# One attention kernel: mixed pairs written where they are used, and W_out's attention rows loaded and split in smaller steps

## The chip, the core and the metric

The kernel runs on one core of a Trainium2 chip. The core has five engines with an instruction queue each: PE (TensorE, matmuls and transposes), DVE (VectorE), ACT (ScalarE), POOL (GpSimd) and SP (SyncE, which here only issues DMA transfers). Each engine takes its instructions in a fixed order and waits on semaphores for the others. The metric is the time of one execution on the device in microseconds; the median of several runs is given.

## What is computed

One layer of a streaming encoder with 1024 tokens of width 1024, in float32: a feed-forward network (FFN), a token mixer, and a second FFN, each followed by a residual layer norm.

```python
x = layer_norm(ALPHA * x + 0.5 * swiglu(x, ffn1...), ln1_g, ln1_b)
z = x @ w_in                       # q, k, v of 8 heads of 64, the gates, the LRU inputs
fox = forgetting_attention(q, k, v, fg)    # softmax(q.k/8 + cum_t - cum_s) v, causal
lru = gelu(...) * rg_lru(causal_depthwise_conv(...), ...)
mix = concatenate([fox, lru]) @ w_out      # w_out: 1024 x 1024, rows 0..511 belong to fox
x = layer_norm(ALPHA * x + mix, ln2_g, ln2_b)
x = layer_norm(ALPHA * x + 0.5 * swiglu(x, ffn2...), ln3_g, ln3_b)
```

The change touches the attention part: how `fox` is kept until it meets `w_out`, and how the four row blocks of `w_out` that belong to it (128 rows of 1024 each) reach the core.

## The kernel before, in words

**Numbers in two parts.** A float32 operand of a matmul is split in a high part (a cast to the matmul's format, on ACT) and a low part (the difference, on DVE), and each product is three matmuls: high by high, high by low, low by high (`mm3`, lines 166 to 168). So every weight row block costs a cast and a subtraction before PE can use it.

**The attention** (`attention`, from line 1363) runs over 64 units. A unit is one head h and one block i of 128 queries. Heads 0 to 5 run one after the other, i from 7 down to 0; heads 6 and 7 are interleaved at the end. The loop counter n of the program counts units, with a few steps after the last. For each unit, `probs` computes scores on PE (lines 1389, 1390), DVE adds the decay and takes the extremum (1395), ACT the exponential (1396); `to_pT`, three units later (two from unit 32 on), transposes the result on PE (1410) and splits it into `pt` by ACT (1414) and DVE (1415); `values`, for two blocks of queries at a time, multiplies it with v on PE (1431), and ACT and DVE add the two halves into the tile `o` (1434, 1435). From head 5 on (`LAST` = 4), the normalisation is done late: DVE takes the reciprocals (1418), POOL copies them into `gate_raw` (1419), PE transposes them (1440), DVE multiplies (1441). The two heads of a pair together fill 128 rows of `o`, and ACT and DVE (for head 5 POOL) split these into the pair's `mix` tiles, high and low (1443, 1444).

**The other work between the units.** Sixteen fill pieces of 12 matmuls (`piece`) multiply the LRU half of the mix with its rows of W_out; they run at n = 1 to 4 and then three to a head, and the last one at n = 35. At the end come sixteen out tiles (`out_tile`, 12 matmuls each), which multiply the four mixed pairs with the attention rows of W_out, add the residual and normalise; the first comes after the first values of head 7. The stretch from n = 36 to the first out tile has neither.

**W_out's attention rows** are loaded at n = 36 by `out_w` (line 1351): two transfers of 1 MB into the two `raw` buffers, two row blocks each. One whole row block is split at each of n = 39, 41, 43, 45 by `split_ws` (lines 158, 159), 128 x 1024 in one cast and one subtraction.

**The mixed pairs** 0, 1 and 3 are written into two tiles of the pool `mxp`, pair 2 into a tile of the pool `hp`. Pairs 0 and 1 are not left there: when they are complete, POOL stores them to device memory (1447), and at n = 40 and 50 SP loads them into `row` buffers (1532), from which the out tiles read.

**Loads of a head.** At block i = 5 of a head (at (6, 6) for the last) SP asks for the next head's q, k, decay row (1059, 1064) and v (1374). There are two v buffers, so v of head h + 1 takes that of head h - 1, which is still being read by its last values for another unit.

**What sets the order.** A scheduler places the recorded instructions on each engine; `issue_after` makes the issue of a transfer stand behind another one on SP. The pools hand out buffers in turn, and an instruction that writes a buffer waits for the last reader of what was there. The FFN that follows (`ready_pair`) loads weights that were prepared earlier (`pre_d`, line 588): two tiles of operands named t4 and t2 into the two `raw` buffers, and smaller ones into new `ws` buffers that become free when the attention is over.

## Time and profile before

| | |
|---|---|
| median of 3 runs | 2314.07 us (2312.58 to 2314.19) |
| the profiled execution | 2308.6 us, of which the span from first to last instruction 2306.8 us |
| busy: PE, DVE, ACT, POOL | 2278.0, 1701.5, 1063.6, 308.4 us |
| granted PE clock | 0.998 |
| attention, first scores to last out tile | about 1163 to 1379 us of the span |

A row of the timeline has the start in us from the span's begin, the duration, the engine, the line of the kernel, the operation, the tile written and the tiles read, and in brackets the idle time of the engine just before and what ended it. Tile names have no buffer numbers: all `raw` buffers are `raw`. Rows with SPq are transfers issued by SP; a row that covers several instructions (x2) gives the time from the first to the last. PE rows overlap, since matmuls are pipelined: a 128x512 matmul is shown with 0.39 us, and the next starts 0.23 us later.

### The profile page before, as it was taken

To read this page: it belongs to the slowest core of one execution; us is meant where nothing else is said; L and a number is where in the kernel's file an instruction comes from. 1 tells how busy PE (TensorE), PEld (TensorE's weight loads), DVE (VectorE), ACT (ScalarE), POOL (GpSimd) and SP (SyncE) were. 2 spreads that over 40 slices of the span, in tenths; PEclk is the share of its full clock that TensorE was granted. 3 is DMA by queue.
4 is the path that set the end of the run, shared out by engine and by line. 5 is a ranking of instruction groups with operands and counts; after the bars stand their busy time and mean duration, and the time that the engine had idled before them with its cause. 6 is when DMAs were issued, how large, how long until landed. Compare 5 with 4: busy or idle time off the path is not lost.

```text
span 2306.8 us, 29448 instructions
## 1 busy us (share of the span) xinstructions
PE 2278.0 (99%) x10609; PEld 1895.0 (82%) x10609; DVE 1701.5 (74%) x2749; ACT 1063.6 (46%) x1771; POOL 308.4 (13%) x503
## 2 busy tenths in 40 slices
PE   9999999999999999999999999999999999999998
PEld 7878888888888888987788788888888888888887
DVE  8878787878467788877767899665656666577886
ACT  5454545454344335455556755333333343344341
POOL 0242323232000001121133200000000000000000
PEclk9999999999999999999999999999999999999999
DMA  4565656565376444366786734232323232564542
GB/s 155 194 212 210 211 207 216 200 223 188 108 271 221 148 142 149 131 205 203 263 249 165 246 119 151 87 119 87 119 87 119 87 119 87 201 251 159 185 144 73
DMA packets 210321, 387.10 MB, mean 168 GB/s; under 512 B 13616, under 2 KB 112240, under 8 KB 210176
## 3 DMA queue, kind: packets, MB, share of 16 engines
q1 hardware_dynamic: 173760, 262.21, 34.8%
q0 software_dynamic: 36416, 123.02, 13.6%
q8 instruction: 83, 1.36, 0.2%
q14 instruction: 62, 0.51, 0.1%
HBM read 258.27 MB, written 126.91 MB: 167 GB/s over the span
## 4 chain that ended last, share of the span: by engine, by line
PE 87%; DVE 4%; issue 4%; DMA 1%; ACT 1%; POOL 1%; SPq 0%; DVEq 0%; POOLq 0%; ACTq 0%
PE x L166 9%; PE x L168 9%; PE x L167 9%; PE b L166 7%; PE b L167 7%; PE b L168 7%; PE a L168 6%; PE a L166 6%; PE a L167 6%; PE s L168 5%; PE s L167 5%; PE s L166 5%; PE a L1431 1%; PE a L1410 1%; PE a L1093 1%
## 5 line engine op out<-in xcount | busy, mean ns | idle before, releaser
L381 ACT CAST ws<-t 128x512 fp32r<-128x512 f32 x240 | 147.7, 623 | 320.4 <-PE b L167 137.8
L382 DVE TENSOR_TENSOR ws<-t,ws 128x512 fp32r<-128x512 f32 x240 | 163.5, 685 | 71.3 <-ACT ws L381 36.2
L167 PE MATMUL a<-ws,ws 128*128 128x512 f32 x512 | 199.8, 390 | 0.6 <-DVE ws L813 0.6
L166 PE MATMUL b<-As,ws 128*128 128x512 f32 x512 | 199.7, 390 | 0.6 <-ACT As L417 0.4
L166 PE MATMUL a<-ws,ws 128*128 128x512 f32 x512 | 199.3, 390 | 0.4 <-ACT row L705 0.4
L167 PE MATMUL b<-As,ws 128*128 128x512 f32 x512 | 199.5, 390 | 0.0
L168 PE MATMUL a<-ws,ws 128*128 128x512 f32 x512 | 199.4, 390 | 0.0
L168 PE MATMUL b<-As,ws 128*128 128x512 f32 x512 | 199.3, 389 | 0.0
L166 PE MATMUL x<-As,ws 128*128 128x512 f32 x504 | 196.5, 390 | 2.8 <-ACT row L686 1.6
L168 PE MATMUL x<-As,ws 128*128 128x512 f32 x504 | 196.2, 389 | 0.0
L167 PE MATMUL x<-As,ws 128*128 128x512 f32 x504 | 196.2, 389 | 0.0
L166 PE MATMUL x<-A,ws 128*128 128x512 f32 x496 | 193.3, 390 | 0.9 <-DVE row L556 0.5
L168 PE MATMUL x<-A,ws 128*128 128x512 f32 x496 | 193.2, 389 | 0.7 <-DVE ws L382 0.7
L381 ACT CAST ws<-raw 128x512 fp32r<-128x512 f32 x180 | 110.7, 622 | 179.7 <-PE x L167 136.3
L167 PE MATMUL x<-A,ws 128*128 128x512 f32 x496 | 193.1, 389 | 0.0
L810 ACT CAST ws<-raw 128x1024 fp32r<-128x1024 f32 x112 | 117.4, 1050 | 160.9 <-PE a L167 80.9
L382 DVE TENSOR_TENSOR ws<-raw,ws 128x512 fp32r<-128x512 f32 x180 | 123.0, 686 | 91.3 <-ACT ws L381 74.3
L740 POOL DMA_DIRECT2D h_d<-row x96 | 69.5, 725 | 857.0 <-DVE row L734 840.4
L813 DVE TENSOR_TENSOR ws<-raw,ws 128x1024 fp32r<-128x1024 f32 x112 | 136.5, 1220 | 48.1 <-ACT ws L810 47.4
L166 PE MATMUL s<-ws,ws 128*128 128x512 f32 x384 | 149.5, 389 | 0.0
L168 PE MATMUL s<-ws,ws 128*128 128x512 f32 x384 | 149.5, 389 | 0.0
L167 PE MATMUL s<-ws,ws 128*128 128x512 f32 x384 | 149.5, 389 | 0.0
(354 smaller groups left out, 5408.9 us busy)
## 6 DMA issues: line engine op xcount, KB each, us to landing
raw<-h_d SPq DMA_DIRECT2D x56, 1024.0 KB, 5.5
h_d<-row POOLq DMA_DIRECT2D x96, 512.0 KB, 3.4
wd<-in_ffn_w_down_dram SPq DMA_DIRECT2D x32, 1024.0 KB, 7.6
raw<-in_ffn_w_gate_dram SPq DMA_DIRECT2D x30, 1024.0 KB, 5.2
raw<-in_ffn_w_up_dram SPq DMA_DIRECT2D x30, 1024.0 KB, 5.2
wq_d<-ws POOLq DMA_DIRECT2D x112, 256.0 KB, 3.8
wq<-wq_d SPq DMA_DIRECT2D x56, 512.0 KB, 3.6
aux<-in_w_in_dram SPq DMA_DIRECT2D x80, 128.0 KB, 3.4
```

The source lines that it names most:

```text
L166: mm(out, ah, bh, start=first, stop=False, skip_group_check=goes_on)
L167: mm(out, ah, bl, start=False, stop=False, skip_group_check=goes_on)
L168: self.last_mm = mm(out, al, bh, start=False, stop=last, skip_group_check=goes_on)
L381: nc.scalar.copy(hi, src)
L382: v.tensor_tensor(lo, src, f32(hi), ALU.subtract)
L740: nc.gpsimd.dma_start(d[:, 2 * n:2 * n + 2], t.rearrange("p (r t) -> p r t", r=2))
L810: cast = nc.scalar.copy(hi, src)
L813: self.mark = v.tensor_tensor(lo, src, f32(hi), ALU.subtract)
L1093: nc.tensor.matmul(pa[:, 0:width], xh, wh[:, 0:width], start=k == 0, stop=False)
L1410: nc.tensor.transpose(pa[:, (j % 4) * P:(j % 4 + 1) * P], p[:, j * P:(j + 1) * P], self.ident)
L1431: mm(pv[:, ps], vt[:, j, :], pts[h, qt][j // 4][l][:, j % 4, ps], start=j == 0 and l == 0, stop=j == last and l == 1)
```

## The change

- Mixed pairs are written where the out tiles read them, and are neither stored nor loaded: pair 0 into a `raw` buffer (taken at the first unit of head 1), pair 1 into `mxp`, pair 2 into `hp` as before, pair 3 into two `row` buffers. The four stores (1447) and the four loads (1532) go.
- W_out's attention rows come at n = 36 in four transfers of 512 KB, one per row block: two into `row` buffers, two into the halves of one `raw` buffer.
- Each row block is split in two halves of 128 x 512, at n = 39, 40, 42, 43, 45, 47, 49 and 51 (`split_out_w`).
- v of the next head is asked for at i = 2 (at (6, 4) for the last head) in place of i = 5; q, k and decay of head 1 at i = 4.
- `ready_pair`'s first loads stand behind the last load of a head in place of the last load of a mixed pair.

```diff
--- before.py
+++ after.py
@@ -589,7 +589,7 @@
                                       ready[both.index(m), OPERANDS.index(n)][:, l].rearrange("p h (k f) -> p h k f", k=2))
                 m.w[n] = to
 
-            with self.tc.issue_after(self.mix_load.ins):
+            with self.tc.issue_after(self.row_load.ins):
                 for n in ("11", "21", "t1"):
                     for m in both:
                         fetch(n, m, two_blocks())
@@ -1348,14 +1348,22 @@
             qk_unit(3, {"t1": [load_heads, split_row], "t3": [split_row, split_row], "22": [split_row]})
         self.last_product = self.last_mm
 
-    def out_w(self, w_out):
-
-        raws = []
-        for c in range(2):
-            raws.append(self.raw([P, 2, D]))
-            with self.tc.issue_after(self.row_load.ins):
-                self.row_load = self.nc.sync.dma_start(raws[c], w_out[2 * c * P:(2 * c + 2) * P, :].rearrange("(f p) d -> p f d", p=P))
-        return [r[:, j:j + 1, :] for r in raws for j in range(2)]
+    def load_out_w(self, w_out, t):
+
+        at = len(self.w_raws) * P
+        with self.tc.issue_after(self.row_load.ins):
+            self.row_load = self.nc.sync.dma_start(t, w_out[at:at + P, :])
+        self.w_raws.append(t)
+
+    def split_out_w(self, to, d):
+
+        if d == 0:
+            to.append(tuple(self.wsp.tile([P, 4 * VW], F32R, tag="ws", name=self.nm("w"))[:, 0:D] for _ in range(2)))
+        ds = slice(d * H, (d + 1) * H)
+        x = self.w_raws[len(to) - 1][:, ds]
+        hi, lo = (t[:, ds] for t in to[-1])
+        self.nc.scalar.copy(hi, x)
+        self.nc.vector.tensor_tensor(lo, x, f32(hi), ALU.subtract)
 
     def attention(self, w_out, mixp, ln, x1_d, normed):
 
@@ -1370,16 +1378,18 @@
                     with self.tc.issue_after(self.row_load.ins):
                         for n in names:
                             self.load_head(h, n)
-                vt = vtp.tile([P, NT, P], F32R, tag="v", name=self.nm("v"))
-                self.row_load = nc.sync.dma_start(f32(vt), self.v_d[h].rearrange("(j p) d -> p j d", p=P))
-                q, kh, kl, cum = (self.heads[n][:, b, :] for n in names)
-                return q, kh, kl, vt, cum
+                return [self.heads[n][:, b, :] for n in names]
+
+            def load_v(h):
+                vts[h] = vtp.tile([P, NT, P], F32R, tag="v", name=self.nm("v"))
+                with self.tc.issue_after(self.row_load.ins):
+                    self.row_load = nc.sync.dma_start(f32(vts[h]), self.v_d[h].rearrange("(j p) d -> p j d", p=P))
 
             sums, inv = self.fgz, self.wf.rearrange("p h i -> p (h i)").rearrange("p (h i) -> p h i", h=HEADS)
 
             def probs(h, i):
 
-                q, kh, kl, _, cum = heads[h]
+                q, kh, kl, cum = heads[h]
                 n = (i + 1) * P
                 ts = slice(i * P, n)
                 s = self.s_tile()
@@ -1420,7 +1430,7 @@
                                           r.rearrange("p b u -> p u b").unsqueeze(3).to_broadcast([P, 2, 2, 64]))
 
             def values(h, qt):
-                vt = heads[h][3]
+                vt = vts[h]
                 b = h % 2
                 rows, rest = slice(64 * b, 64 * b + 64), slice(64 - 64 * b, P - 64 * b)
                 pv = self.a_tile()
@@ -1442,17 +1452,14 @@
                     hi, lo = (x[:, cols] for x in mixes[h // 2])
                     nc.scalar.copy(hi, t[:, cols])
                     (nc.gpsimd if LAST < h < HEADS - 1 else v).tensor_tensor(lo, t[:, cols], f32(hi), ALU.subtract)
-                    if qt == 0 and h < 5:
-                        for l in range(2):
-                            nc.gpsimd.dma_start(mix_d[h // 2][l], f32(mixes[h // 2][l]))
-
-            heads, pts, ps, outs, mixes = {}, {}, {}, {}, {}
-            mix_d = [self.dram.tile([2, P, T], F32, name=f"mix{c}_d") for c in range(2)]
+
+            heads, vts, pts, ps, outs, mixes = {}, {}, {}, {}, {}, {}
             units = [(h, i) for h in range(HEADS - 2) for i in reversed(range(NT))]
             units += [(6 + h, i) for h, i in ((0, 7), (0, 6), (0, 5), (0, 4), (1, 7), (1, 6), (0, 3), (0, 2),
                                               (1, 5), (1, 4), (0, 1), (0, 0), (1, 3), (1, 2), (1, 1), (1, 0))]
-            tiles, mix, w_fox = [], [], []
-            MIXES = 40, 50
+            self.w_raws = []
+            tiles, w_fox = [], []
+            SPLITS = 39, 40, 42, 43, 45, 47, 49, 51
             fill = [(i, d) for i in range(NT) for d in range(2)]
             AHEAD, LAST = 3, 4
 
@@ -1476,6 +1483,7 @@
             PIECES = {0: 0, 1: 1, 2: 2}
             with self.tc.issue_after(self.row_load.ins):
                 heads[0] = load(0)
+            load_v(0)
             open_row(0)
             open_row(1)
 
@@ -1485,7 +1493,7 @@
 
             def out_tile():
                 i, d = tiles.pop(0)
-                self.down_tile(i, list(zip(mix + [mixes[2], mixes[3]], w_fox)), (d,))
+                self.down_tile(i, list(zip([mixes[c] for c in range(4)], w_fox)), (d,))
                 if d:
                     self.layer_norm(i)
                     normed(i)
@@ -1493,17 +1501,21 @@
             for n in range(len(units) + AHEAD + 1):
                 if n < len(units):
                     h, i = units[n]
-                    if i == 5 and h < 6 or (h, i) == (6, 6):
+                    if i == (5 if h else 4) and h < 6 or (h, i) == (6, 6):
                         heads[h + 1] = load(h + 1)
+                    if i == 2 and h < 6 or (h, i) == (6, 4):
+                        load_v(h + 1)
                     if i == NT - 1:
                         if h % 2 == 0:
                             outs[h // 2] = tp.tile([P, T], F32, tag="o", name=self.nm("o"))
                         else:
-                            if h == 5:
-                                t = self.hp.tile([P, 2, T], F32R, tag="w2", name=self.nm("mix"))
-                                mixes[2] = t[:, 0, :], t[:, 1, :]
+                            if h == 3:
+                                mixes[1] = tuple(mixp.tile([P, T], F32R, tag="h", name=self.nm("mix")) for _ in range(2))
+                            elif h == 7:
+                                mixes[3] = tuple(self.rowp.tile([P, T], F32R, tag="row", name=self.nm("mix")) for _ in range(2))
                             else:
-                                mixes[h // 2] = tuple(mixp.tile([P, T], F32R, tag="h", name=self.nm("mix")) for _ in range(2))
+                                t = (self.rawp if h == 1 else self.hp).tile([P, 2, T], F32R, tag="raw" if h == 1 else "w2", name=self.nm("mix"))
+                                mixes[h // 2] = t[:, 0, :], t[:, 1, :]
                     with self.tc.issue_after(self.last_product.ins):
                         ps[n], scores = probs(h, i)
                 for m in due(n):
@@ -1520,16 +1532,14 @@
                 if n in ROWS:
                     open_row(ROWS[n])
                 if n == 36:
-                    w_raws = self.out_w(w_out)
-                if 39 <= n < 47 and n % 2:
-                    w_fox.append(tuple(t[:, 0, :] for t in self.split_ws(w_raws[len(w_fox)], 1)))
+                    raw = self.raw([P, 2, D])
+                    for t in (self.row(), self.row(), raw[:, 0, :], raw[:, 1, :]):
+                        self.load_out_w(w_out, t)
+                if n in SPLITS:
+                    self.split_out_w(w_fox, SPLITS.index(n) % 2)
                 if n == 52:
                     t = self.hp.tile([P, 2, T], F32, tag="w3", name=self.nm("gb"))
                     self.load_gb(*ln, [t[:, l, :] for l in range(2)])
-                if n in MIXES:
-                    mix.append(tuple(self.rowp.tile([P, T], F32R, tag="row", name=self.nm("mix")) for _ in range(2)))
-                    for l in range(2):
-                        self.mix_load = nc.sync.dma_start(f32(mix[-1][l]), mix_d[len(mix) - 1][l])
                 if tiles:
                     out_tile()
             return tiles, out_tile
```

How this moves instructions, at the three places that matter for what follows.

ACT, at the first split of a row block of W_out; `w` is the high part, `pt` the transposed probabilities, `p` the probabilities. Before:

```order
L1414 CAST pt_11631<-a_11635 128x4x128
L1396 ACTIVATE p_11624,fgz<-p_11624,m_11628 128x512
L1414 CAST pt_11633<-a_11642 128x2x128
L1434 COPY o_11463<-a_11647 64x256
L158 CAST w_11741<-raw_11666 128x1024
L1396 ACTIVATE p_11673,fgz<-p_11673,m_11677 128x384
L1414 CAST pt_11631<-a_11680 128x4x128
```

Now:

```order
L1424 CAST pt_11622<-a_11626 128x4x128
L1365 CAST w_11737<-row_11658 128x512
L1406 ACTIVATE p_11615,fgz<-p_11615,m_11619 128x512
L1424 CAST pt_11624<-a_11633 128x2x128
L1365 CAST w_11737<-row_11658 128x512
L1444 COPY o_11458<-a_11638 64x256
L1365 CAST w_11834<-row_11659 128x512
L1424 CAST pt_11622<-a_11676 128x4x128
```

A half cast stands right behind the first pt cast, ahead of the exponential of 512; three half casts are done before the third pt cast, where one whole cast was.

DVE, at the last subtractions of W_out; `wfr` holds the reciprocals, ISA is the decay step. Before:

```order
L1418 RECIPROCAL wfr<-fgz 128x2x2
L159 TENSOR_TENSOR w_11952<-raw_11668,w_11951 128x1024
L1441 TENSOR_TENSOR o_11463<-o_11463,a_11922 128x256
L1415 TENSOR_TENSOR pt_11888<-a_11938,pt_11887 128x4x128
L1415 TENSOR_TENSOR pt_11890<-a_11945,pt_11889 128x128
L1395 ISA p_11958,m_11962<-s_11955,cum_10168 128x256
L1395 ISA m_11962 128x1
L1415 TENSOR_TENSOR pt_11966<-a_11967,pt_11965 128x4x128
L1395 ISA p_11998,m_12002<-s_11995,cum_10168 128x128
L1395 ISA m_12002 128x1
L1418 RECIPROCAL wfr<-fgz 128x2x2 x2
L1435 TENSOR_TENSOR o_11463<-o_11463,a_11974 64x256
```

Now:

```order
L1366 TENSOR_TENSOR w_11944<-raw_11657,w_11943 128x512
L1451 TENSOR_TENSOR o_11458<-o_11458,a_11912 128x256
L1425 TENSOR_TENSOR pt_11878<-a_11930,pt_11877 128x4x128
L1425 TENSOR_TENSOR pt_11880<-a_11937,pt_11879 128x128
L1405 ISA p_11950,m_11954<-s_11947,cum_10168 128x256
L1405 ISA m_11954 128x1
L1425 TENSOR_TENSOR pt_11958<-a_11959,pt_11957 128x4x128
L1405 ISA p_11990,m_11994<-s_11987,cum_10168 128x128
L1405 ISA m_11994 128x1
L1428 RECIPROCAL wfr<-fgz 128x2x2
L1366 TENSOR_TENSOR w_12070<-raw_11657,w_12069 128x512
L1428 RECIPROCAL wfr<-fgz 128x2x2
```

In the place of the whole subtraction behind the first reciprocal is a half; the last row block's first half stands lower, between the two reciprocals that were together, and its second half comes right behind the second of them.

SP, at the load of W_out; `q`, `kh`, `kl`, `cum` and `v` are loads of a head. Before:

```order
L1059 DMA cum_10168<-cum_d 128x1024
L1374 DMA v_11521<-v_d 128x8x128
L1357 DMA raw_11666<-in_w_out_dram 128x2x1024
L1357 DMA raw_11668<-in_w_out_dram 128x2x1024
L1532 DMA mix_11776<-mix_d 128x1024
L1532 DMA mix_11777<-mix_d 128x1024
L1064 DMA q_10161<-q_d 64x1024 x2
L1064 DMA kh_10162<-k_d 64x1024 x2
L1064 DMA kl_10167<-k_d 64x1024 x2
L1059 DMA cum_10168<-cum_d 128x1024
```

Now:

```order
L1059 DMA cum_10168<-cum_d 128x1024
L1355 DMA row_11658<-in_w_out_dram 128x1024
L1355 DMA row_11659<-in_w_out_dram 128x1024
L1355 DMA raw_11657<-in_w_out_dram 128x1024 x2
L1386 DMA v_11664<-v_d 128x8x128
L1064 DMA q_10161<-q_d 64x1024 x2
L1064 DMA kh_10162<-k_d 64x1024 x2
L1064 DMA kl_10167<-k_d 64x1024 x2
L1059 DMA cum_10168<-cum_d 128x1024
L1386 DMA v_11918<-v_d 128x8x128
L105 DMA gb_12194<-in_ln_g_dram 128x1024
L108 DMA gb_12194<-in_ln_b_dram 128x1024
```

The v load that stood ahead of W_out stands behind it, W_out is four transfers, the loads of the mixed pairs are gone, and the layer norm's `gb` comes ahead of the last head's loads.

## The prediction

> **What bounds the kernel now.** I read the page's busy times first, then the attention stage cut into windows (busy time of each engine in each stretch), because the whole change lies there.
>
> ```profile
> PE 2278.0 (99%) x10609; PEld 1895.0 (82%) x10609; DVE 1701.5 (74%) x2749; ACT 1063.6 (46%) x1771; POOL 308.4 (13%) x503
> ```
>
> ```profile
> core 0: us, PE busy (x) PEld busy (x) DVE busy (x) ACT busy (x) POOL busy (x), PEclk, DMA share, GB/s
> 1180.00:1262.00 82.00, 81.01 (x508) 71.76 (x508) 62.54 (x167) 51.22 (x125) 30.91 (x61) 1.00 0.61 170
> 1272.25:1296.00 23.75, 19.41 (x136) 16.22 (x134) 20.62 (x47) 20.41 (x46) 5.41 (x12) 1.00 0.98 325
> 1304.00:1319.00 15.00, 14.08 (x94) 11.59 (x95) 13.23 (x31) 13.45 (x32) 3.80 (x11) 1.00 0.71 265
> 1319.00:1363.00 44.00, 43.85 (x238) 36.90 (x237) 40.26 (x96) 24.22 (x50) 5.32 (x13) 1.00 0.12 49
> ```
>
> TensorE (PE) is busy 2278.0 of 2306.8 us, so a change that leaves its work alone can win 28.8 us at most. From 1180 to 1262, with the fill pieces, PE lacks 0.99 us in 82; from 1319, with the out tiles, 0.15 in 44. Between them it lacks 23.75 - 19.41 = 4.34 us in 1272.25 to 1296, and 0.92 in 1304 to 1319. In the first of these two, VectorE (DVE) and ScalarE (ACT) are both at about 87% and the DMA engines at 0.98: here W_out's attention rows are loaded and split. All of PE's idle time there is 0.19% of the kernel.
>
> Next, the chain of waits (start, length, what):
>
> ```profile
> 1269.16 6.63 DMA raw<-in_w_out_dram
> ...
> 1294.43 0.86 DVE w L159
> ```
>
> The load of W_out is on the chain itself from 1269.16 for 6.63 us, and the last subtraction of its split (L159) is on it again at 1294.43. So the change works on something that sets the end, but what it can win there is small.
>
> **The change part by part.** The matmuls are the same in number and size, so PE's busy time stays. What moves is when ACT and DVE get to the splits. Their present order, from the timeline (idle time before an instruction, and its releaser, in brackets), ACT first:
>
> ```profile
> 1272.32 0.59 ACT L1414 CAST pt<-a 128x512 fp32r<-128x512 f32 x1 [1.77 <-PE a L1410]
> 1272.81 0.72 ACT L1396 ACTIVATE p<-p,m 128x512 f32<-128x512 f32 x1
> 1273.44 0.19 ACT L1396 ACTIVATION_READ_ACCUMULATOR p<-p,m 128x1 f32 x1
> 1273.54 0.35 ACT L1414 CAST pt<-a 128x256 fp32r<-128x256 f32 x1
> 1274.43 0.37 ACT L1434 COPY o<-a 64x256 f32<-64x256 f32 x1 [0.55 <-PE a L1431]
> 1275.87 1.05 ACT L158 CAST w<-raw 128x1024 fp32r<-128x1024 f32 x1 [1.06 <-DMA raw<-in_w_out_dram]
> ```
>
> ```profile
> 1272.94 0.69 DVE L1415 TENSOR_TENSOR pt<-a,pt 128x512 fp32r<-128x512 f32 x1 [0.22 <-ACT pt L1414]
> 1273.92 0.42 DVE L1415 TENSOR_TENSOR pt<-a,pt 128x256 fp32r<-128x256 f32 x1 [0.29 <-ACT pt L1414]
> 1274.89 0.56 DVE L1395 CUSTOM_DVE_ANT_0 p<-s,cum 128x384 f32<-128x384 f32 x1 [0.54 <-PE s L1390]
> ...
> 1286.55 1.19 DVE L159 TENSOR_TENSOR w<-raw,w 128x1024 fp32r<-128x1024 f32 x1
> ...
> 1298.64 0.18 DVE L1418 RECIPROCAL wfr<-fgz 128x4 f32<-128x4 f32 x1 [0.53 <-ACT p L1396]
> 1299.03 0.42 DVE L1435 TENSOR_TENSOR o<-o,a 64x256 f32<-64x256 f32 x1 [0.21 <-ACT o L1434]
> ```
>
> And the view of L159 alone (min/median/max ns, first and last start; what its waits were for: us in all, times):
>
> ```profile
> L159 DVE TENSOR_TENSOR w<-raw,w x4: 1185/1209/1225, 1276.9 to 1294.4; 128x1024 fp32r<-128x1024 f32 x4
> ...
>   ACT w L158: 0.9, 2
> ```
>
> A half split does not stand in this stretch, but its two forms run in the FFN stages (groups by line and form: count, busy us, mean ns):
>
> ```profile
> L382 DVE TENSOR_TENSOR ws<-raw,ws 128x512 fp32r<-128x512 f32 x180 | 123.0, 686 | 91.3 <-ACT ws L381 74.3 <-PE b L167 9.2 <-issue 3.3
> ...
> L381 ACT CAST ws<-raw 128x512 fp32r<-128x512 f32 x180 | 110.7, 622 | 179.7 <-PE x L167 136.3 <-PE x L168 38.1 <-issue 1.6
> ```
>
> A half costs DVE 0.69 and ACT 0.62 us: two halves 1.38 and 1.24, against 1.21 and 1.05 for a whole row block. How long a load takes from issue to landing there, in the last column (transfers issued between 1268.5 and 1277):
>
> ```profile
> raw<-in_w_out_dram SPq DMA_DIRECT2D x2, 1024.0 KB, 8.0
> mix_d<-mix POOLq DMA_DIRECT2D x2, 512.0 KB, 8.2
> mix<-mix_d SPq DMA_DIRECT2D x2, 512.0 KB, 11.1
> v<-v_d SPq DMA_DIRECT2D x1, 512.0 KB, 3.8
> ```
>
> *Term 1, row blocks 0 and 1 (DVE from 1272.94 on).* The first load still goes out at about 1269.2, since the last fill piece must leave its new home, as it had to leave the second of the old ones, but it is 512 KB and no v load goes ahead of it. I take the 3.8 us of v, which had this size and this place in the queue: 1273.0. In the new order the first half cast stands right behind the pt cast that ends at 1272.91, so ACT waits 0.1 us where it waited 1.06. DVE now waits 0.29 + 0.54 + 0.9 = 1.75 us in all. In the new order it waits for the first half, ready at 1273.0 + 0.62 = 1273.62, when its pt ends at 1273.63 (0); for the small pt, ready after the exponential, its read and the cast at 1273.62 + 0.72 + 0.19 + 0.35 = 1274.88, when DVE is free at 1274.32 (0.55); and for the second half at 1275.5, when it is free at 1275.3 (0.2). That is 0.75 us of waits and 2 x (1.38 - 1.21) = 0.34 of added work: 0.75 + 0.34 - 1.75 = **-0.7 us**. Bounds: no wait left, -1.4; the load as late as today's first, +2.1 (a rival below).
>
> *Terms 2 and 3, the subtractions at 1286.55 and 1294.43.* In both places now stands a half: 1.2 - 0.7 = **-0.5 us** each. Bounds: 0 where DVE then waits for ACT or PE instead, -0.5 where it does not. I take the full value, since DVE is on the chain at 1294.43 and shows no wait ahead of either.
>
> *Term 4, the last row block's two halves.* They stand behind the reciprocals of the last two rows above, where DVE idles 0.53 + 0.21 us: 1.38 - 0.74 = **+0.6 us**. Bounds 0 and +1.4.
>
> *Edits costed at nothing.* The four stores and four loads of mixed pairs go: PE waits for none of them, only the DMA queues get emptier. v is asked for three units later. The waits of the SP queue and two PE rows bear on this and on the raw buffer that mixed pair 0 now holds:
>
> ```profile
> SPq L1374 <- PE a L1431: 30.7, 5, 8.3
> ```
>
> ```profile
> 1376.90 0.40 PE L168 MATMUL a<-w,mix 128*128 128x512 f32 x1
> ```
>
> ```profile
> L166 PE MATMUL x<-As,raw x8: 389/390/390, 1405.6 to 1410.4; 128*128 128x512 f32 x8
> ```
>
> SP stood 30.7 us for v's buffer, with x1 rows, W_out or the next head behind it, and PE waited for none of these but W_out. v still comes seven units ahead of its first use, five for the last head; the window from 1272.25 holds ten units (2.4 us each), so five are 12 us, against 3.8 to land. The raw buffer is free only after the third matmul of the last out tile (1376.90), so the second raw load of the FFN behind cannot go out at 1306 as now. It would land about 10 us later, at 1387 or by the slowest landing above at 1390; PE first reads that tile at 1405.6. The cover is 15 us; without it PE would stand for what is missing.
>
> Behind 1304 the order on ACT, DVE and PE differs in details up to the first out tile. I put 0, with -0.9 (all of PE's idle time there) and +0.9 as bounds.
>
> **Sum**: -0.7 - 0.5 - 0.5 + 0.6 = **-1.1 us**. The profiled execution took 2308.6 us (1.8 around its span), so its like would take 2307.5. The median of the runs shown, 2314.07, lies 5.5 us above it; the forecast for the median is 2314.07 - 1.1 = **2313.0 us**.
>
> **A lock between POOL and DVE.** While the subtraction of 1286.55 runs, a POOL instruction stretches:
>
> ```profile
> 1286.60 1.29 POOL L1393 TENSOR_SCALAR_AFFINE_SELECT cum<-cum 128x128 f32<-128x128 f32 x1 [1.48 <-DVE m L1395]
> 1287.84 0.39 POOL L1419 COPY gate_raw<-wfr 128x256 f32<-128x256 f32 x1
> 1290.65 0.29 POOL L1393 TENSOR_SCALAR_AFFINE_SELECT cum<-cum 128x128 f32<-128x128 f32 x1 [2.42 <-DVE m L1395]
> ```
>
> The select took 1.29 instead of 0.29, up to the end of the subtraction. POOL lost there, which costs nothing. In the new order the last two halves each stand right behind a reciprocal whose result POOL copies: if the copy comes first, DVE may stand for its 0.39 us, twice, +0.8.
>
> The Trainium skill, "SBUF — State Buffer", section "Who interferes with whom", says that a DVE instruction with two SBUF inputs and a GpSimd instruction that reads SBUF lock each other out, and that the order of issue decides which one stands. By that rule the side on which DVE loses is as open as the other; the rows show the lock, and only POOL losing.
>
> **The rivals.**
> - *The splits leave the chain altogether* (chance 0.20). For it: load and subtraction are on the chain, and the stretches without them lack far less. Against: DVE and ACT are at 87% there and get more work. All 4.34 us gone: 2309.7.
> - *ACT stands on the row earlier than before* (0.15; slower). The first half cast is now ahead of an exponential and a pt cast, and the values wait for these. If the 512 KB land when the 1 MB did, at 1275.8, ACT stands 2.9 us instead of 0.1: -1.1 + 2.8 = +1.7, or 2315.8. It turns slower from a landing 1.1 us later than mine, 4.9 us after the issue; at the 11.1 us of the mix loads it would be +6. Against: a v load and 2 MB of mix traffic leave these queues.
> - *POOL's copies come first* (0.10): -1.1 + 0.8 = -0.3, or 2313.8.
> - *Nothing is saved* (0.10): the waits come back as waits for PE or ACT, and the 0.17 us that each of four row blocks adds remain: +0.7, or 2314.8.
>
> **How the numbers follow.** The forecast has 0.45. The range takes in the first rival and the slower one, the latter with the bounds of term 4 and of the part behind 1304 partly on top: 2309.5 to 2317.0. 0.2% is 4.6 us, about what runs of this kernel can tell from no change. The first rival gets there only with the idle time behind 1304 too, 0.09 for faster; the slower one needs a landing later than 9 us, 0.07; within it 0.84.
>
> **What would show it.** In the changed profile: the first half cast (w<-row) waits under 0.5 us for its DMA, whose row lands in about 4 us; PE lacks about 1 us less between the last fill piece and the first out tile; the two last halves on DVE start at once behind their reciprocals, or some 0.4 us later. I am wrong if ACT shows one wait of over 1 us on W_out's rows, if PE waits at the first products of the second FFN, or if PE lacks more than today's 0.15 us under the out tiles.

## The result, and the profile after

| | before | changed kernel |
|---|---|---|
| median | 2310.59 us (20 runs, 2307.90 to 2314.19) | 2306.92 us (20 runs, 2304.89 to 2310.66) |
| ratio | | 0.9984, 95% interval 0.9978 to 0.9991 |
| the profiled execution, its span | 2308.6, 2306.8 us | 2306.02, 2304.3 us |

The change makes the kernel faster by 3.7 us by the medians (2.1 to 5.1 by the interval), which is less than 0.2%. The forecast was 2313.0 with a range from 2309.5: the time lies below the range. Two different things went wrong, and the traces separate them: the median that the forecast was hung on, and the size of the gain.

The 20 runs of the kernel before include the three that were shown. These (2312.58 to 2314.19) lay in the upper part of what it does. Two of the later sets hold the changed kernel as it is:

| set | before, 33 runs | changed kernel, 11 runs | ratio |
|---|---|---|---|
| second | 2308.96 us | 2307.37 us | 0.9994 (0.9985 to 1.0003) |
| third | 2309.01 us | 2307.23 us | 0.9992 (0.9983 to 1.0001) |

The changed kernel's median hardly moves between the sets (2306.92, 2307.37, 2307.23); that of the kernel before does (2310.59, 2308.96, 2309.01). So the medians alone put the gain anywhere between 1.6 and 3.7 us, and the profile has to say how large it is.

**Where the time went.** PE's busy time is the same as before:

```profile
PE 2278.2 (99%) x10609; PEld 1894.2 (82%) x10609; DVE 1702.2 (74%) x2753; ACT 1063.8 (46%) x1775; POOL 305.7 (13%) x499
```

I therefore count PE's idle time in the stretch that the change touches: from the last matmul of the last fill piece to the first matmul of the first out tile. I cut it where PE has been busy for 20.00 us since its start, so that the two parts hold nearly the same work in every kernel, as long as PE's granted clock is the same (two kernels below are an exception). Windows (window, its length, PE busy, then PEld, DVE, ACT, POOL, clock, DMA share, GB/s), first of the kernel before, then of the changed one:

```profile
1271.00:1294.59 23.59, 20.00 (x139) 16.84 (x138) 20.07 (x47) 19.30 (x44) 5.15 (x13) 1.00 1.04 345
1294.59:1321.58 26.99, 24.88 (x171) 21.10 (x170) 24.04 (x56) 21.30 (x51) 8.46 (x20) 1.00 0.68 217
```

```profile
1270.41:1292.21 21.80, 20.00 (x139) 16.77 (x138) 19.45 (x49) 19.46 (x48) 4.08 (x11) 1.00 0.91 283
1292.21:1318.70 26.49, 24.65 (x170) 20.57 (x168) 24.26 (x57) 20.83 (x50) 7.74 (x19) 1.00 0.49 140
```

Before, PE lacks 23.59 - 20.00 = 3.59 us in the first part and 2.11 in the second, 5.70 in all. After, it lacks 1.80 and 1.84, 3.64 in all. The change saves **2.06 us**, 1.79 of it in the first part. Two further profiles of the changed kernel lack 3.72 and 3.64 us, so this measure repeats within 0.1 us, where whole runs spread over 6 us.

The spread of whole runs comes from elsewhere. Two places that no edit of this study touches vary from profile to profile: the first 400 us (PE lacks 6.3 to 8.5 us there) and 1020 to 1180 us, up to the first head's first scores (4.0 to 7.1 us). The extremes of the second place are both kernels of the experiments below, aft_whole_after and aft_whole_again (windows, columns as above):

```profile
1020.00:1180.00 160.00, 156.04 (x680) 126.15 (x679) 115.25 (x192) 89.54 (x134) 28.47 (x49) 0.99 0.74 249
```

```profile
1020.00:1180.00 160.00, 152.90 (x667) 123.01 (x666) 114.20 (x191) 88.41 (x132) 28.43 (x49) 1.00 0.74 246
```

That is 3.1 us between two programs that are the same up to there (in the first, the granted clock was 0.55 from 1166.5 to 1170, so that its PE did less in its busy time; the lowest at full clock there is bef_halves with 4.1). So one profile's span says nothing about a change of 2 us; idle time of PE between two points of the program does.

**The start of the stretch, after.** The transfers of W_out's first row block (KB, us from issue to landing), and SP's waits from 1255 to 1272 (us, times, longest):

```profile
row<-in_w_out_dram SPq DMA_DIRECT2D x1, 512.0 KB, 3.5
```

```profile
SPq L1355 <- PE a L168: 10.5, 2, 9.0
```

The row was issued at 1268.54, after SP had stood 9.0 us for a `row` buffer that the last fill pieces read, and was there at 1272.0. ACT's timeline (start, duration; idle time before in brackets, where there is any to speak of):

```profile
1271.73 0.59 ACT L1424 CAST pt<-a 128x512 fp32r<-128x512 f32 x1 [1.77 <-PE a L1420]
1272.21 0.62 ACT L1365 CAST w<-row 128x512 fp32r<-128x512 f32 x1
1272.73 0.73 ACT L1406 ACTIVATE p<-p,m 128x512 f32<-128x512 f32 x1
1273.36 0.19 ACT L1406 ACTIVATION_READ_ACCUMULATOR p<-p,m 128x1 f32 x1
1273.45 0.36 ACT L1424 CAST pt<-a 128x256 fp32r<-128x256 f32 x1
1273.70 0.63 ACT L1365 CAST w<-row 128x512 fp32r<-128x512 f32 x1
```

ACT does not wait for W_out at all, here or later. And DVE's timeline, at the first two halves and at the last two:

```profile
1272.96 0.68 DVE L1366 TENSOR_TENSOR w<-row,w 128x512 fp32r<-128x512 f32 x1
1273.84 0.43 DVE L1425 TENSOR_TENSOR pt<-a,pt 128x256 fp32r<-128x256 f32 x1 [0.20 <-ACT pt L1424]
1274.37 0.69 DVE L1366 TENSOR_TENSOR w<-row,w 128x512 fp32r<-128x512 f32 x1
1274.97 0.41 DVE L1445 TENSOR_TENSOR o<-o,a 64x256 f32<-64x256 f32 x1
1275.31 0.54 DVE L1405 CUSTOM_DVE_ANT_0 p<-s,cum 128x384 f32<-128x384 f32 x1
...
1295.05 0.17 DVE L1428 RECIPROCAL wfr<-fgz 128x4 f32<-128x4 f32 x1
1295.13 0.66 DVE L1366 TENSOR_TENSOR w<-raw,w 128x512 fp32r<-128x512 f32 x1
1295.76 0.18 DVE L1428 RECIPROCAL wfr<-fgz 128x4 f32<-128x4 f32 x1
1295.85 0.81 DVE L1366 TENSOR_TENSOR w<-raw,w 128x512 fp32r<-128x512 f32 x1
```

### The profile page after: what moved, and what is told of

It is laid out like the page before. It is cut to its first block, busy times and chain, and to the rows that moved or that the text cites. A ratio compares the mean times of both kernels' runs of the same rounds, so it can differ in the third digit from the quotient of the medians.

```text
span 2304.3 us, 29440 instructions
## 1 busy us (share of the span) xinstructions
PE 2278.2 (99%) x10609; PEld 1894.2 (82%) x10609; DVE 1702.2 (74%) x2753; ACT 1063.8 (46%) x1775; POOL 305.7 (13%) x499
## 4 chain that ended last, share of the span: by engine, by line
PE 79%; issue 8%; DVE 6%; POOL 2%; DMA 2%; ACT 2%; SPq 0%; DVEq 0%; POOLq 0%; ACTq 0%
PE x L166 8%; PE x L168 8%; PE x L167 8%; PE a L168 6%; PE a L167 6%; PE a L166 6%; PE b L167 6%; PE b L166 6%; PE b L168 6%; PE s L167 4%; PE s L168 4%; PE s L166 4%; PE a L1441 1%; POOL wq_d L285 1%; PE a L1420 1%
```

## The experiments

Two theories went in. **The early row**: W_out's first row block is there when ACT wants it, and this, with the halved subtractions, is the gain. **Rivals**: emptier DMA queues (the mixed pairs' 4 MB are gone), halving alone, or v's place. All edits are small; the tables and texts use the names of the runs. "Lacks" is PE's idle time in the stretch, as first part + second part.

| kernel | lacks, us | length of the stretch, us | ratio of the time to before (95%) |
|---|---|---|---|
| before | 3.59 + 2.11 = 5.70 | 50.58 | 1 |
| changed kernel | 1.80 + 1.84 = 3.64 | 48.29 | 0.9984 (0.9978 to 0.9991) |
| after_again, after_third | 3.72, 3.64 | 48.42, 48.28 | 0.9994, 0.9992 |
| aft_traffic | 1.77 + 1.83 = 3.60 | 48.24 | 0.9991 (0.9983 to 1.0000) |
| aft_vearly | 1.80 + 1.99 = 3.79 | 48.26 | 0.9987 (0.9978 to 0.9995) |
| aft_whole_spread | 1.82 + 2.15 = 3.97 | 48.83 | 0.9992 (0.9983 to 1.0001) |
| bef_halves | 1.95 + 1.79 = 3.74 | 48.70 | 0.9988 (0.9979 to 0.9997) |
| aft_whole, aft_whole_again | 1.94 + 0.56 = 2.50, 2.57 | 47.42, 47.52 | 0.9980 (0.9971 to 0.9989), 0.9981 (0.9972 to 0.9990) |
| aft_halves_early | 3.34 + 0.69 = 4.03, at a lower clock | 49.83 | 0.9995 (0.9987 to 1.0004) |
| aft_whole_after | 1.74 + 2.28 = 4.02 | 49.14 | 0.9991 (0.9982 to 1.0000) |
| bef_vlate | 3.06 + 1.24 = 4.30 | 49.10 | 0.9990 (0.9981 to 0.9999) |
| bef_all_but_pairs | 2.38 + 1.13 = 3.51, at a lower clock | 49.22 | 0.9995 (0.9986 to 1.0003) |

The intervals of the ratios, some 2 us to each side, overlap nearly everywhere. The idle time is what tells the kernels apart. Each edit also makes the scheduler place instructions anew, so a run shows an edit together with the order that came of it; in some orders two or four matmuls of the scores are done ahead of the stretch, and then its length counts them as saved and the idle time does not.

Idle time compares two kernels only at the same clock. In two profiles the granted clock fell in the first part. Its windows, first of aft_halves_early, then of bef_all_but_pairs, with one microsecond of the latter:

```profile
1270.45:1293.79 23.34, 20.00 (x126) 16.90 (x125) 20.46 (x48) 18.45 (x45) 3.69 (x11) 0.93 0.82 257
```

```profile
1270.06:1292.44 22.38, 20.00 (x131) 17.42 (x129) 20.20 (x48) 18.38 (x44) 5.26 (x12) 0.92 1.00 311
1278.06:1279.06 1.00, 1.00 (x6) 1.00 (x6) 0.98 (x6) 0.99 (x3) 0.29 (x1) 0.50 1.17 398
```

PE did 126 and 131 matmuls in its 20.00 us, where the other kernels did 136 to 139. Over the whole stretch both hold the same matmuls as before, aft_whole_spread, bef_halves and aft_whole_after, whose PE is busy 44.86 to 45.12 us; theirs is busy 45.81 and 45.71. So in the terms of the other kernels they lose 0.7 to 0.95 and 0.6 to 0.85 us more than they lack: I put aft_halves_early at 4.7 to 5.0 us and bef_all_but_pairs at 4.1 to 4.4 (estimates from these figures).

### The mixed pairs' traffic put back: aft_traffic

```diff
+                    if qt == 0 and h < 5:
+                        for l in range(2):
+                            nc.gpsimd.dma_start(mix_d[h // 2][l], f32(mixes[h // 2][l]))
...
+                if n in (40, 50):
+                    for l in range(2):
+                        nc.sync.dma_start(spare_d[n // 50][l], mix_d[n // 50][l])
```

> The changed kernel, with the traffic of the old mixed pairs put back and nothing read from it: four stores of 512 KB on POOL's queue at the old places, and at units 40 and 50 four copies of 512 KB on SP's queue in place of the old loads. The order of instructions on TensorE, ScalarE and VectorE is that of the changed kernel. Theory (the gain comes from W_out's first row arriving before ScalarE wants it, and from halved subtractions): between the last fill piece and the first out tile TensorE lacks 3.65 us as in the changed kernel, within 0.4, and the time is that of the changed kernel, 3 to 4 us below the kernel before. Rival (the emptier DMA queues bring the gain): W_out's first row lands 6 us or more after its issue in place of 3.5, ScalarE stands over 1.5 us for it, TensorE lacks 5 us or more, and at least half of the 3.7 us is lost.

It lacks 3.60 us, like the changed kernel, with the order of its instructions unchanged. (Its time lies 1.8 us below the kernel before and not 3 to 4; the level of the kernel before was lower in this set.) Not all of the traffic came back where it had been: the copies of the first pair went out at 1232.82, ahead of the stretch, and in the first part the DMA moved 326 GB/s, where the kernel before has 345 and the changed kernel 283. But bef_halves, below, has all of it (333 GB/s) and lacks only 3.74 us. So the emptier queues bring nothing that is seen here.

### v asked for early again: aft_vearly

```diff
-                    if i == (5 if h else 4) and h < 6 or (h, i) == (6, 6):
+                    if i == 5 and h < 6 or (h, i) == (6, 6):
                         heads[h + 1] = load(h + 1)
-                    if i == 2 and h < 6 or (h, i) == (6, 4):
                         load_v(h + 1)
```

> The changed kernel with v asked for with its head, three units earlier, as in the kernel before; so v of the sixth head goes ahead of W_out's rows in SP's queue. The order on ScalarE and VectorE differs from the changed kernel in one place: both halves of row block 0 stand together, behind the exponential of 512 and the small pt. Theory: W_out's first row lands about 2 us later after the last fill piece (v's 512 KB at the 340 GB/s of that stretch are 1.5 us, and its issue 0.5), ScalarE stands 0.3 to 1 us for it, TensorE lacks 0.3 to 1 us more than the 3.65, and so does the time. Rival (the order of v does not matter): ScalarE does not stand for W_out and TensorE lacks 3.65 us within 0.2.

It lacks 3.79 us, 0.15 more than the changed kernel and 0.07 more than the highest of its three profiles; the theory had asked for 0.3 to 1. v went out at 1267.37 and W_out's rows at 1267.88, 1.87 us ahead of the last matmul of the last fill piece (1269.75); in the changed kernel they go at 1268.54, also 1.87 us ahead of it (1270.41). So v delayed W_out's issue by nothing: SP stands for the row buffer until then in any case. The row took 4.6 us to land in place of 3.5, but in this order its first cast stands behind the exponential (1272.54), and ACT does not wait for it. The stretch is no longer than in the changed kernel (48.26 us against 48.28 to 48.42). In the changed kernel v's place is worth next to nothing. (It is worth something where a buffer is free: bef_vlate, below.)

### One part alone: the early row, and the halves

The early row without halves: aft_whole_spread has the changed loads, but whole splits that stand where the kernel before has them.

```diff
-                if n in SPLITS:
-                    self.split_out_w(w_fox, SPLITS.index(n) % 2)
+                if 39 <= n < 47 and n % 2:
+                    cast, less = self.split_out_w(w_fox)       # a whole row block
+                    if n == 43:
+                        self.issue_behind(less, decs[5, 5])    # decay instruction of 768
+                    if n == 45:
+                        self.issue_behind(cast, exps[5, 5])
+                        self.issue_behind(less, decs[5, 2])    # decay instruction of 384
```

> The changed kernel with whole splits, the third and fourth subtraction held where the kernel before has them: behind the reciprocals that follow the decay instructions of 768 and 384 of the sixth head. Loads, v and mixed pairs stay changed, so against the kernel before only the earlier row acts. Theory: the earlier row is worth 0.8 to 1.3 us (VectorE reached the 1024 decay instruction 0.8 us and the reciprocal 1.3 us earlier in the changed kernel): TensorE lacks 4.4 to 4.9 us, against 5.70 before, and the time is 0.7 to 1.4 us below the kernel before. Rival (the earlier row is worth nothing by itself, since halves with the old loads lacked as little as the changed kernel): 5.5 us or more.

And the halves without the early row: bef_halves is the kernel before with the split of the changed one (two loads of 1 MB, behind v).

```diff
-                if 39 <= n < 47 and n % 2:
-                    w_fox.append(tuple(t[:, 0, :] for t in self.split_ws(w_raws[len(w_fox)], 1)))
+                if n in SPLITS:                                # 39, 40, 42, 43, 45, 47, 49, 51
+                    ...                                        # as split_out_w of the change
```

> The kernel before with one edit: W_out's row blocks are split in halves at units 39, 40, 42, 43, 45, 47, 49 and 51. Two loads of 1 MB, v ahead of them, and the stores and loads of the mixed pairs stay. Theory: the first cast still stands for the 1 MB (about 1 us on ScalarE), so of the change's gain only the halvings come, about -1.0 + 0.6 us: TensorE lacks 5.0 to 5.6 us between the last fill piece and the first out tile (5.70 in the kernel before), and the time is 0.1 to 0.7 us below the kernel before. Rival (halving is all of the gain): TensorE lacks 3.65 us and the time is 2 us or more below the kernel before.

Windows, first of aft_whole_spread, then of bef_halves, with the one long wait of bef_halves' ACT:

```profile
1272.55:1294.37 21.82, 20.00 (x136) 16.68 (x135) 19.28 (x45) 18.64 (x42) 4.90 (x10) 1.00 0.92 283
1294.37:1321.38 27.01, 24.86 (x174) 21.41 (x173) 24.60 (x58) 21.95 (x53) 8.82 (x21) 1.00 0.50 137
```

```profile
1271.48:1293.43 21.95, 20.00 (x137) 16.56 (x135) 18.77 (x46) 18.25 (x44) 4.38 (x12) 1.00 1.04 333
1293.43:1320.18 26.75, 24.96 (x172) 21.24 (x172) 25.55 (x60) 22.42 (x55) 8.56 (x21) 1.00 0.78 250
```

```profile
1276.57 0.62 ACT L1532 CAST w<-raw 128x512 fp32r<-128x512 f32 x1 [1.29 <-DMA raw<-in_w_out_dram]
```

Both expectations missed, on the same side. The early row alone saves 1.73 us (5.70 to 3.97; 0.8 to 1.3 was expected), all of it in the first part. The halves alone save 1.96 (0.1 to 0.7 was expected), though ACT still stands 1.29 us for the 1 MB: the delay is there (PE has lost 1.40 us when it has done 10 us of work, the changed kernel 1.05), and is made up by the time that 20 us are done. Together the two save 2.06. **The parts do not add.** Either of them brings the first part from 3.59 to between 1.8 and 2.0 us, and the other then finds nothing left there; the second part keeps about 2 us in all of these kernels. Why the halves alone make good the late row is not shown.

### What remains: place and size of the splits

Undoing the halving altogether was meant to cost. aft_whole is the changed kernel with one whole split at each of n = 39, 41, 43, 45:

```diff
-            SPLITS = 39, 40, 42, 43, 45, 47, 49, 51
...
-                if n in SPLITS:
-                    self.split_out_w(w_fox, SPLITS.index(n) % 2)
+                if 39 <= n < 47 and n % 2:
+                    self.split_out_w(w_fox)                    # a whole row block
```

> The changed kernel with W_out's row blocks split whole, one each at units 39, 41, 43 and 45 as in the kernel before; loads, v and mixed pairs stay changed. Theory: the early row keeps its gain (1.3 us on VectorE by the trace), the two halvings (0.5 us each) go, and the 0.6 us of the last row block and the added work of halves (0.17 for each row block) are saved: TensorE lacks 3.9 to 4.7 us between the last fill piece and the first out tile, and the time lies 0.3 to 1 us above the changed kernel. Rival (halving and its later places are all of the gain): TensorE lacks 5.5 us or more, the time is that of the kernel before. Rival (halving brings nothing, load and queues do it all): TensorE lacks 3.65 us or less.

It gains: 2.50 us lacking, and the lowest median of its set, 2305.31. In the issue order all four whole subtractions now stand ahead of the 1024 decay instruction of head 5, where only four of the eight halves stood. Its windows, and DVE's row with the last two:

```profile
1271.86:1293.80 21.94, 20.00 (x137) 16.75 (x135) 20.33 (x46) 18.43 (x41) 3.90 (x10) 1.00 0.89 280
1293.80:1319.28 25.48, 24.92 (x175) 21.15 (x173) 23.34 (x57) 21.55 (x53) 7.99 (x21) 1.00 0.52 145
```

```profile
1280.14 2.38 DVE L1364 TENSOR_TENSOR w<-raw,w 128x1024 fp32r<-128x1024 f32 x2
```

The first part now holds all four splits, where that of aft_whole_spread holds three; it lacks only 0.12 us more. The second part, now free of splits, lacks 0.56 in place of 2.15. I repeated it beside the changed kernel in one set:

> The changed kernel with whole splits at units 39, 41, 43 and 45, once more, beside the changed kernel itself in the same set. If what it lacks between the last fill piece and the first out tile (2.50 against 3.64 us in the first profiles) is its own and not chance of one profile: 2.4 to 2.6 again, and a median 0.6 to 1.7 us below that of the changed kernel in this set. If chance: 3.6, and the same median within 0.4.

> The changed kernel itself, as the other side of that comparison: TensorE lacks 3.6 to 3.8 us in the stretch, the median lies 1.5 to 2.6 us below the kernel before.

> The changed kernel as it is, once more, beside its relatives. Between the last fill piece and the first out tile TensorE lacks 3.64 us again, within 0.1; what differs from its first profile lies in the first 400 us and at the start of the first head (1020 to 1180 us), where the profiles so far differ by 2.0 and 2.6 us without any edit there. Its time lies 2.1 us below the kernel before (what the stretch gives), within 1, if the 3.7 us first measured held a difference between the sets of runs; 3.7 us below it if the change saves something outside the stretch.

aft_whole_again lacks 2.57 us, and its median is 2305.02 us against 2307.23 of the changed kernel: 2.2 us less, more than the 0.6 to 1.7 that were expected, but 0.8 to 3.7 by resampling the two times 11 runs. The idle time accounts for 1.07 of these. **aft_whole is faster than both kernels.** The two repetitions of the changed kernel lie 1.6 and 1.8 us below the kernel before, nearer to the stretch's 2.06 than to 3.7, though their intervals alone reach from 0.7 us slower to 3.9 us faster.

From aft_whole I formed a new theory: only the place counts, DVE is full from the 1024 decay instruction to the last reciprocal of head 5, and any split work taken out of there is saved. Two kernels test it from both sides, eight halves in the early place and whole splits behind that stretch.

```diff
+                if n == 39:                                    # aft_halves_early
+                    for j in range(8):
+                        last = self.split_out_w(w_fox, j % 2)
+                if n == 40:
+                    self.issue_behind(decs[5, 7], last)        # decay instruction of 1024, head 5
```

> The changed kernel with its eight halves kept, but all of them issued ahead of the first decay instruction of the sixth head (128x1024 on VectorE), so in the place that the four whole splits took when they were undone. Theory (the place counts: VectorE is full from that decay instruction to the last reciprocal of the sixth head, 94% in the kernel before, and split work taken out of that stretch is saved, work ahead of it falls partly into VectorE's waits): TensorE lacks 2.5 us, as with whole splits there, and up to 0.7 more for the 0.17 us that each row block in halves adds, so 2.5 to 3.2, and the time is 0.4 to 1.1 us below the changed kernel. Rival (the size counts, halves serve the chain worse than whole ones wherever they stand, or nothing but chance of the order): 3.64 us or more.

```diff
+                if n in (39, 41, 48, 51):                      # aft_whole_after
+                    cast, less = self.split_out_w(w_fox)       # a whole row block
+                    if n == 48:
+                        self.issue_behind(cast, exps[5, 0])
+                        self.issue_behind(less, decs[6, 7])
+                    if n == 51:
+                        self.issue_behind(cast, exps[6, 6])
+                        self.issue_behind(less, decs[6, 5])
```

> The changed kernel with whole splits, the first two early as in the other whole kernel, the third and fourth subtraction held back behind the decay instructions of 1024 and of 640 of the seventh head, so behind the stretch in which VectorE is full. Theory (any place outside that stretch serves): TensorE lacks 2.2 to 3.2 us between the last fill piece and the first out tile. Rival (only the early place serves, where VectorE waits for ScalarE and for scores anyway; later each whole split delays a decay instruction that scores or values wait for): 3.6 us or more.

The theory fell on both sides: 4.03 us (4.7 to 5.0 with the lower clock) and 4.02. Behind the full stretch two whole splits cost the second part as much (2.28) as in it. And the halves forced into the early place clear the second part (0.69), but the first part lacks 1.5 us more than without force, and loses some 0.8 us to the clock on top. DVE's rows there, and the longest of PE's waits in the first part (us, times, longest):

```profile
1281.14 1.88 DVE L1366 TENSOR_TENSOR w<-raw,w 128x512 fp32r<-128x512 f32 x3
1282.95 1.21 DVE L1405 CUSTOM_DVE_ANT_0 p<-s,cum 128x1024 f32<-128x1024 f32 x1
```

```profile
PE s L1399 <- DVE m L1405: 1.9, 1, 1.9
```

PE stood 1.9 us for the 1024 decay instruction, which frees the buffer that the next scores go into, because three halves had been put ahead of it; behind this wait, from 1284.6 to 1288.0, the granted clock was 0.50. In aft_whole this wait is not among PE's waits. There the scheduler placed splits and matmuls together; here I held one instruction back, and the order of PE's matmuls had not been made for it. That this is the difference between 2.50 and 4.03 is read from the two traces; no run isolates it.

### v's place in the kernel before, and all but the pairs

bef_vlate makes one edit to the kernel before, the later request for v; bef_all_but_pairs makes all edits but the final places of the pairs.

```diff
+                    if i == 2 and h < 6 or (h, i) == (6, 4):   # both kernels: v out of load()
+                        load_v(h + 1)
...
-                self.row_load = self.nc.sync.dma_start(raws[c], w_out[2 * c * P:(2 * c + 2) * P, :]...)
+            for j in range(2):                                 # bef_all_but_pairs only, with SPLITS in halves
+                with self.tc.issue_after(self.row_load.ins):
+                    self.row_load = self.nc.sync.dma_start(raws[c][:, j, :], w_out[(2 * c + j) * P:(2 * c + j + 1) * P, :])
```

> The kernel before with one edit: v is asked for with the unit of 384 columns, three units later, as in the changed kernel, so no v stands ahead of W_out in SP's queue. The mixed pairs go out and come back, W_out comes in two loads of 1 MB and is split whole at the old units. SP stood 8.3 us for v's buffer ahead of W_out, and the first of the two raw buffers was not waited for, so the first 1 MB can go at about 1260, right behind the head's rows, where the changed kernel's first row waited 9.0 us for a row buffer of the last fill pieces. The order now has the first cast ahead of the pt cast that follows the last fill piece, and all four whole splits ahead of the 1024 decay instruction. Theory (what counts is that W_out's first rows are there when the last fill piece ends): the first 1 MB lands before 1270, ScalarE does not stand for it, TensorE lacks 2.0 to 2.8 us in the stretch (5.70 before), and the time is 2 to 3.5 us below the kernel before: the request for v alone gives all of the gain. Rival (the slower one of the prediction: a cast that stands ahead of the pt cast waits for a load that lands 6.6 us after 1269): ScalarE stands 3 us or more, TensorE lacks 7 us or more, the time is 1.5 us or more above the kernel before.

> The kernel before with all edits of the change but one: v later, W_out in four loads of 512 KB (into the two raw buffers), split in eight halves at units 39 to 51; the mixed pairs of heads 0 to 3 still go out and come back. Theory (pairs in their final places bring nothing by themselves, and cost the buffer into which W_out's first rows could have gone early): W_out's first two rows land before 1270, TensorE lacks 2.0 to 3.6 us in the stretch, so no more than the changed kernel's 3.64. Rival (pairs in place carry part of the gain): 4.2 us or more.

Of bef_vlate, SP's timeline, and ACT's row of the third cast:

```profile
1259.62 0.39 SPq L1357 DMA_DIRECT2D raw<-in_w_out_dram  x1
...
1270.64 0.38 SPq L1357 DMA_DIRECT2D raw<-in_w_out_dram  x1
```

```profile
1277.13 1.05 ACT L158 CAST w<-raw 128x1024 fp32r<-128x1024 f32 x1 [1.90 <-DMA raw<-in_w_out_dram]
```

The first 1 MB goes at 1259.62, as expected, 9 us earlier than in the changed kernel, and its casts wait for nothing. But the second one must wait for the last fill piece and lands 6.5 us after 1270.64, and the third cast stands 1.90 us for it. Neither side of the expectation holds: it lacks 4.30 us, 1.40 less than the kernel before and 1.80 more than aft_whole, which issues its four whole subtractions ahead of the same decay instruction and waits for no load. The slower rival of the prediction exists, then, as a wait of 1.9 us, but on the third row block, and its price is paid out of a larger gain.

bef_all_but_pairs lacks 3.51 us, which looks like no more than the changed kernel, and like the theory. But its stretch is 0.93 us longer (49.22 us), and with the lower clock counted it is at 4.1 to 4.4 us, about where its rival begins. ACT's row of the third row block, and PE's wait that came of it:

```profile
1275.13 1.14 ACT L1538 CAST w<-raw 128x512 fp32r<-128x512 f32 x2 [1.26 <-DMA raw<-in_w_out_dram]
```

```profile
1276.93 0.39 PE L1434 MATMUL a<-pt,v 128*128 128x256 f32 x1 [1.89 <-ACT pt L1417]
```

W_out's first two rows were there early, as in bef_vlate, and as there ACT stood for the next ones, 1.26 us; a `pt` cast came behind, PE stood 1.89 us for it, and from 1277.5 to 1280.5 the granted clock was 0.50. So the run does not show that the pairs in their final places bring nothing. They take one of the two `raw` buffers, into which W_out's first rows could go 9 us earlier; but the changed kernel, whose first rows go into `row` buffers, has no wait of ACT for W_out. Its loss is 0.5 to 0.7 us smaller, and the medians (2307.88 against 2307.23 us in the same set) do not decide it.

## Why the prediction was wrong, point by point

- **"The median of the runs shown, 2314.07, lies 5.5 us above it; the forecast for the median is 2314.07 - 1.1."** This step failed first, and it is the larger part of the miss. Three runs were taken as the kernel's level; with 20 runs it is 2310.59, and 2309.0 to 2309.4 in three later sets of 33. The sentence before it, by the profiled execution, had given 2307.5; measured are 2306.92 to 2307.37.
- **The sum, -1.1 us.** The stretch gives -2.06. The sign and the places were right, the size was not.
- **Term 1, -0.7.** Counted ahead of the halves, this is the mis-sized term: the early row alone measures -1.73 (aft_whole_spread). Two things were too small in it. First, ACT: counted from the last matmul of the last fill piece, the first half starts at 1.80 us (1272.21 - 1270.41) where the step had 2.0, since the row took 3.5 us in place of 3.8; and from its start to the end of the small pt cast ACT takes 1.60 us (1272.21 to 1273.81), where the step added full durations, 0.62 + 0.72 + 0.19 + 0.35 = 1.88. The durations of successive rows overlap. So DVE waits 0.20 us for the small pt and 0.1 for the second half, where the step has 0.55 + 0.2. Second, the step stopped counting at the first two row blocks. To the 1024 decay instruction DVE is 0.79 us faster than before (9.61 for 10.40) with one addition of `o` (0.33 us) done more, so 1.1; to the reciprocal behind it, where both have done the same, 1.30 us faster (1284.56 - 1270.41 = 14.15 for 1286.45 - 1271.00 = 15.45); and the wait of 0.49 us for ACT ahead of DVE's pt at 1288.82 is gone as well (the next wait of that size in the changed kernel, 0.51 us at 1290.41, is for PE).
- **Terms 2, 3 and 4, -0.5 - 0.5 + 0.6 = -0.4.** On top of the early row the halves measure -0.33 (3.97 to 3.64), so the sum of the three is right, by luck of the order in which they are counted: on the old loads they measure -1.96 (bef_halves), and the early row on top of them only -0.10 (3.74 to 3.64). So which term was mis-sized depends on the order; the step that failed in either is the sum. It assumed that the terms add, and they do not.
- **Term 4's mechanism** is right in place: the two last halves stand behind the reciprocals, and the first took 0.66 us, the second 0.81.
- **POOL's copies first (the rival at 0.10)** happened at one of the two last halves, with the copy of the reciprocal before, and cost less than its 0.4 us. POOL's timeline:

```profile
1292.31 0.67 POOL L1429 COPY gate_raw<-wfr 128x256 f32<-128x256 f32 x1 [0.64 <-DVE wfr L1428]
...
1295.72 0.40 POOL L1429 COPY gate_raw<-wfr 128x256 f32<-128x256 f32 x1 [1.00 <-PE a L1450]
```

The copy at 1292.31 began while an earlier half of DVE ran (1292.07, 0.66 us) and took 0.67 in place of 0.40. The copy at 1295.72 began first, and the half of 1295.85 took 0.81 in place of 0.66: DVE lost 0.15 us, less than the 0.27 us of the copy that were left. By the rule of the Trainium skill, "SBUF — State Buffer", section "Who interferes with whom", the order of issue decides which of the two stands; these two rows agree, one for each side.
- **Edits at nothing.** Right for the stores and loads of the mixed pairs as far as aft_traffic (3.60 against 3.64 us) shows, and nearly for v in this kernel (0.15 at most). Not shown for the places of the pairs: without them bef_all_but_pairs stands at 4.1 to 4.4. Wrong for v in the kernel before: there its load stands ahead of W_out, and its later request alone saves 1.40 us. The weights of the FFN behind, t2 in the raw buffer, were late as said and covered as said. Their issues and PE's reads, changed kernel (count, min/median/max ns, first and last start):

```profile
L588 SPq DMA_DIRECT2D raw<-pre_d x8: 320/430/520, 1302.8 to 1376.1; - x8
...
L166 PE MATMUL x<-As,raw x8: 389/389/389, 1403.0 to 1407.8; 128*128 128x512 f32 x8
```

The last of them goes at 1376.1 and PE reads at 1403.0, with no wait there.
- **Behind 1304, nothing.** Right: from the first values of head 6 (1309.48 before, 1308.02 after) to the first out tile PE lacks 0.19 us before and 0.21 after; from 1304 to there it lacks 0.73 before, and 0.72 after from the like place (1301); and under the out tiles up to 1364 it lacks 0.15 in both.
- **The rivals.** "The splits leave the chain altogether" is not what happened (3.64 us of 5.70 are left, and the chain still runs through ACT's casts of W_out), but it is what aft_whole comes nearer to: 2.5 us. "ACT stands on the row earlier" did not happen in the changed kernel; it did in bef_vlate and bef_all_but_pairs, on the third row block. "Nothing is saved" is out.
- **"What would show it"**: the first half cast waits under 0.5 us (it does not wait), the row lands in about 4 us (3.5), both held; PE lacking about 1 us less did not (2.06).

What stays open: why the kernel before had a median 1.2 to 1.6 us higher in the first 20 runs than in the later sets; why the second part lacks little only when all splits are issued ahead of the 1024 decay instruction (0.5 to 0.7 us in aft_whole, aft_whole_again and aft_halves_early, 1.24 in bef_vlate), while whole splits behind the full stretch cost as much as in it; why the halves alone gain as much as the early row; and what the places of the pairs are worth by themselves.

## What to carry to other kernels

A gain of 2 us in 2300 is smaller than the spread of single runs, so set a forecast on the level of many runs or on the profiled execution, and measure a change by the idle time of the bounding engine between two points of the program: here that repeated within 0.1 us. Look at the granted clock and the length of the stretch beside it, since at half the clock the same work counts as more busy time and hides a loss. Where two edits relieve the same stretch, do not take it that their terms add: here each alone gave nearly all of the gain, since the second finds what the first has left. A transfer that an engine waits for is cured by what lets it be issued earlier (which buffer, behind which other request), and when it is cured look at the next row block: the wait may only have moved there.

## What the runs showed of the hardware that was not expected

- PE waits of 1.9 us were followed by some 3 us at half the granted clock: in aft_halves_early (1.91 us up to 1284.22; 0.50 from 1284.6 to 1288.0) and in bef_all_but_pairs (1.89 us up to 1276.93; 0.50 from 1277.5 to 1280.5). Not every such wait was: in aft_whole_again PE stood 2.77 us up to 1167.85, and the clock stayed at 1.00. What decides is not shown.
- Transfers of one size in one run landed after different times. W_out's first and second 1 MB in bef_vlate, issued at 1259.62 (behind the next head's rows) and at 1270.64 (followed by v and the loads of a mixed pair); what makes the difference is not shown (KB, us from issue to landing):

```profile
raw<-in_w_out_dram SPq DMA_DIRECT2D x1, 1024.0 KB, 9.2
```

```profile
raw<-in_w_out_dram SPq DMA_DIRECT2D x1, 1024.0 KB, 6.5
```

- The lock between POOL and DVE reaches DVE too: 0.66 us became 0.81 when POOL's copy had begun first (one instance, in the changed kernel at 1295.85).
